# Loads and stores of a row softmax as two transfers each, of the even and of the odd partitions

## The chip, the core and the metric

The kernel runs on one core of a Trainium2 chip. The core has engines of its own for different work: VectorE (DVE in the profile), ScalarE (ACT), GpSimd (POOL) and SyncE (SP), which here does nothing but issue transfers and wait. Data moves between the large memory (DRAM, or HBM) and the core's on-chip memory, which has 128 partitions, by 16 DMA engines. The metric is the time of one execution on the device in microseconds; the number that counts is the median of several executions.

## What is computed

A softmax over the last axis of a float32 tensor of 16 x 1024 x 512, so 16384 rows of 512 numbers each:

```python
def reference(x):
    x_max = np.max(x, axis=-1, keepdims=True)
    exp_x = np.exp(x - x_max)
    return exp_x / np.sum(exp_x, axis=-1, keepdims=True)
```

The input is 33.55 MB and so is the output. Nothing can be kept on the chip from one execution to the next, so 67.11 MB have to be moved.

## The kernel before

**Tiles.** A "group" is 8 softmax rows in each of the 128 partitions: 128 x 4096 float32, 2 MB. There are 16 groups (`GROUPS`). The on-chip memory holds a ring of 12 groups (`ring`), and group g lives at place g % 12. Beside it stand two small tiles: `stat`, which holds the negated row maximum and later the row's sum, and `recip`, its reciprocal.

**Transfers.** `LOADS` and `STORES` both say that a transfer moves two groups, 4 MB. There are 8 loads (L0 to L7) and 8 stores (S0 to S7). `in_dram` gives the piece of DRAM that belongs to a transfer: 2048 consecutive softmax rows, which are dealt to the partitions in order, 16 rows to each. So partition p has one run of 32 KB in memory, and the runs of the 128 partitions follow one another. All transfers are issued on SP's queue (`load` in line 127, `store` in line 131).

**Order on SP.** The first six loads are issued at once; the very first is moved ahead of the start barrier (`AT_HEAD`, `loads_at_the_head`). Then the string `ORDER` rules: S0 S1 L6 L7 S2 S3 S4 S5 S6 S7. A store waits until both of its groups are scaled (semaphore `scaled[k]`). L6 and L7 write over places of the ring that S0 and S1 have read, so they wait for the landing of these stores (semaphore `stored[k]`). The last line on SP waits for the landing of all other stores (`others`).

**A landing.** Each transfer adds 16 to its semaphore by the time that it has landed. Line 144 makes DVE wait for 16 on `loaded[k]` before it reads the groups of load k.

**Compute.** The string `SEQUENCE` is the order on DVE, and on POOL. `M3` is the row maximum of group 3, `MM4` that of groups 4 and 5 in one instruction (line 145). `D3` is the scaling of group 3 on DVE, `P4` that of group 4 on POOL: a reciprocal on DVE (line 159), then a multiply (line 161), whose engine is chosen by the letter. ACT runs a loop over the groups (line 134): for each of the 8 rows, an exponential with the sum of the row beside it. Each row is worked on inside its partition; nothing crosses partitions.

Of the kernel before, what the change touches and what calls it, by code (L numbers as in the profile page):

```python
# [15 lines left out]
GROUP = 8  # L16
# [4 lines left out]
STORES = [2, 2, 2, 2, 2, 2, 2, 2]  # L21
GROUPS = sum(LOADS)
LOAD_AT = [sum(LOADS[:k]) for k in range(len(LOADS))]
STORE_AT = [sum(STORES[:k]) for k in range(len(STORES))]

ORDER = """
S0 S1 L6 L7 S2 S3 S4 S5 S6 S7
# [32 lines left out]
@with_exitstack  # L60
def kernel(
    ctx: ExitStack,
    tc: tile.TileContext,
    x: bass.AP,
    out: bass.AP,
):
    nc = tc.nc
    nc.at_finalize(loads_at_the_head)
    P = nc.NUM_PARTITIONS

    x_rows, out_rows = x.flatten_outer_dims(), out.flatten_outer_dims()
    d = x_rows.shape[1]
    assert x_rows.shape[0] == P * GROUPS * GROUP

    def sbuf(name, n):
        return ctx.enter_context(nc.sbuf_tensor(name, [P, n], F32))

    ring = sbuf("ring", RING * GROUP * d)

    stat = sbuf("stat", RING * GROUP)  # L80
    recip = sbuf("recip", RING * GROUP)

    def sem(name):
        return ctx.enter_context(nc.semaphore(name))

    maxima, summed, inverted = [sem(s) for s in ("maxima", "summed", "inverted")]
    loaded = [sem(f"loaded{k}") for k in range(len(LOADS))]
    scaled = [sem(f"scaled{k}") for k in range(len(STORES))]

    def load_of(g):  # L90
        return max(k for k in range(len(LOADS)) if LOAD_AT[k] <= g)

    def store_of(g):
        return max(k for k in range(len(STORES)) if STORE_AT[k] <= g)


    before = {
        k: store_of(LOAD_AT[k] + LOADS[k] - 1 - RING)
        for k in range(len(LOADS))
        if LOAD_AT[k] >= RING  # L100
    }

    awaited = sorted(set(before.values()))
    stored = {k: sem(f"stored{k}") for k in awaited}
    others = sem("others")

    def at(g):
        return g % RING

    def rows(g, groups=1):  # L110
        part = ring[:, at(g) * GROUP * d : (at(g) + groups) * GROUP * d]
        return part.rearrange("p (r d) -> p r d", d=d)

    def cols(t, g, groups=1):
        return t[:, at(g) * GROUP : (at(g) + groups) * GROUP]

    def in_dram(t, g, groups):
        k = load_of(g)
        assert load_of(g + groups - 1) == k
        part = t[P * GROUP * LOAD_AT[k] : P * GROUP * (LOAD_AT[k] + LOADS[k]), :]  # L120
        first = (g - LOAD_AT[k]) * GROUP
        part = part.rearrange("(p r) d -> p r d", p=P)
        return part[:, first : first + groups * GROUP, :]

    def load(k):
        g, n = LOAD_AT[k], LOADS[k]
        return nc.sync.dma_start(out=rows(g, n), in_=in_dram(x_rows, g, n))

    def store(k):
        g, n = STORE_AT[k], STORES[k]  # L130
        return nc.sync.dma_start(out=in_dram(out_rows, g, n), in_=rows(g, n))

    def exp(row, one):
        return nc.scalar.activation(  # L134
            out=row, in_=row, func=EXP, bias=one, scale=1.0, accum_out=one
        )

    def spread(t):
        return t.unsqueeze(2).to_broadcast([P, GROUP, d])


    def rowmax(g, groups):
        assert load_of(g) == load_of(g + groups - 1)
        nc.vector.wait_ge(loaded[load_of(g)], 16)  # L144
        nc.vector.reduce_max(  # L145
            out=cols(stat, g, groups), in_=rows(g, groups), axis=AX, negate=True
        ).then_inc(maxima, groups)

    def exps():
        with nc.Fori(0, GROUPS, 1, engines=(ACT,)) as g:  # L150
            nc.scalar.wait_ge(maxima, 1).then_inc(maxima, -1)  # L151
            row = nc.scalar.snap((g % RING) * GROUP)
            for r in range(GROUP):
                done = exp(ring[:, bass.ds((row + r) * d, d)], stat[:, bass.ds(row + r, 1)])
            done.then_inc(summed, 1)

    def scale(g, engine):
        nc.vector.wait_ge(summed, g + 1)
        nc.vector.reciprocal(out=cols(recip, g), in_=cols(stat, g)).then_inc(inverted, 1)  # L159
        engine.wait_ge(inverted, g + 1)  # L160
        engine.tensor_mul(  # L161
            out=rows(g), in0=rows(g), in1=spread(cols(recip, g))
        ).then_inc(scaled[store_of(g)], 1)

    def done_by(k):
        later = [a for a in awaited if a >= k]
        return stored[later[0]] if later else others

    def store_scaled(k):
        nc.sync.wait_ge(scaled[k], STORES[k])  # L170
        store(k).then_inc(done_by(k), 16)


    with tc.manual_schedule(engines={SP}):
        for k in range(min(before)):
            first = load(k).then_inc(loaded[k], 16)
            tc.info.no_tile_sem_insts.add(first.ins.name)
    tc.close()
    tc.compile()  # L179

    nc.scalar.preload_act_table(EXP)  # L181
    exps()
    for work in SEQUENCE.split():
        kind = work.rstrip("0123456789")
        g = int(work[len(kind) :])
        if kind in ("M", "MM"):
            rowmax(g, len(kind))
        else:
            scale(g, nc.vector if kind == "D" else nc.gpsimd)
    for transfer in ORDER.split():  # L190
        k = int(transfer[1:])
        if transfer[0] == "S":
            store_scaled(k)
        else:
            last = before[k]
            since = max([a for a in awaited if a < last], default=-1)
            nc.sync.wait_ge(stored[last], 16 * (last - since))
            load(k).then_inc(loaded[k], 16)
    nc.sync.wait_ge(others, 16 * (len(STORES) - 1 - max(awaited)))
    nc.sync.nop()  # L200


# [28 lines left out]
```

## Time and profile before

| what | us |
|---|---|
| median of 3 runs (159.95 to 160.03) | 160.0 |
| the profiled execution, its own time | 160.08 |
| its span, from the first to the last instruction | 158.8 |
| DVE busy | 121.8 |
| ACT busy | 92.2 |
| POOL busy | 42.3 |
| row maximum of one group on DVE (L145) | 4.42 |
| row maximum of two groups on DVE | 8.65 |
| multiply of one group on DVE, median (L161) | 4.425 |
| multiply of one group on POOL (L161) | 7.016 |
| one exponential on ACT (L134), of 128 x 512 | 0.707 |
| issue to landing, median: loads, stores | 25.9, 24.0 |

How to read it: a time "busy" is the sum over an engine's instructions. The span is cut into 40 equal slices for the row of digits, where 9 means that an engine (or the 16 DMA engines in the mean) was busy for 90% or more of the slice. From issue to landing counts the wait in the queue behind earlier transfers too, so it is not how long a transfer takes. A DMA packet here is one row of 32 KB of one partition, or a small one at the end of a transfer.

### The profile page before, as it was taken

How to read it: one execution, taken by the hardware profiler on the slowest of the kernel's cores; microseconds unless marked ns; L12 is line 12 of the kernel's file. 1: busy time of each engine (PE TensorE's matmuls, PEld its weight loads, DVE VectorE, ACT ScalarE, POOL GpSimd, SP SyncE). 2: the span in 40 equal slices, each digit the busy share in tenths (PEclk: the TensorE clock that was granted, in tenths of full speed). 3: DMA queues.
4: the chain of work that ended last, by engine and by line, in shares of the span. 5: the costliest groups of instructions: out<-in, count | busy, mean ns of one | idle time of the engine just before them, and what ended most of it. 6: DMA issues, size and time to landing. Idle time of an engine off the chain costs nothing.

```text
span 158.8 us, 572 instructions
## 1 busy us (share of the span) xinstructions
DVE 121.8 (77%) x36; ACT 92.2 (58%) x257; POOL 42.3 (27%) x10
## 2 busy tenths in 40 slices
DVE  0008979999999999999999499999999999700000
ACT  0300699969406999999988990899599300000000
POOL 0000000000007903930970790079049300000000
DMA  7999999999999999999999999999999999999996
GB/s 264 438 479 405 405 495 421 396 438 471 413 405 438 471 405 396 396 413 471 438 396 462 446 413 405 454 421 438 438 421 446 413 446 438 438 421 438 429 429 264
DMA packets 2304, 67.11 MB, mean 423 GB/s; under 512 B 256, under 2 KB 256, under 8 KB 256
## 3 DMA queue, kind: packets, MB, share of 16 engines
q1 hardware_dynamic: 2304, 67.11, 98.9%
HBM read 33.55 MB, written 33.55 MB: 423 GB/s over the span
## 4 chain that ended last, share of the span: by engine, by line
DMA 45%; DVE 39%; issue 2%; DVEq 0%
DMA ring<-in_x_dram 26%; DVE ring L161 22%; DMA out_dram<-ring 20%; DVE stat L145 16%; DVE recip L159 1%; DVEq L144 0%
## 5 line engine op out<-in xcount | busy, mean ns | idle before, releaser
L134 ACT ACTIVATE ring<-ring,stat x128 | 90.4, 707 | 28.1 <-ACTq L151 28.1
L145 DVE TENSOR_REDUCE stat<-ring 128x16 f32<-128x8192 f32 (+1 forms) x10 | 69.5, 6956 | 15.7 <-DMA ring<-in_x_dram 15.7
L161 POOL TENSOR_TENSOR ring<-ring,recip 128x4096 f32<-128x4096 f32 x6 | 42.1, 7016 | 81.8 <-DVE recip L159 81.8
L161 DVE TENSOR_TENSOR ring<-ring,recip 128x4096 f32<-128x4096 f32 x10 | 51.1, 5109 | 0.3
L134 ACT ACTIVATION_READ_ACCUMULATOR ring<-ring,stat x128 | 23.8, 186 | 0.0
L181 ACT ACT_TABLE_LOAD x1 | 1.3, 1283 | 4.0 <-PEq L179 4.0
L159 DVE RECIPROCAL recip<-stat 128x8 f32<-128x8 f32 x16 | 3.0, 190 | 0.0
L215 POOL MEMSET const-float32-0.0<- 128x1 f32 x1 | 0.1, 98 | 0.2 <-issue 0.2
L215 POOL MEMSET const-bfloat16-1.0<- 128x1 bf16 x1 | 0.1, 102 | 0.0
L215 POOL MEMSET const-uint8-127<- 128x1 uint8 x1 | 0.1, 102 | 0.0
L215 POOL MEMSET const-float32-1.0<- 128x1 f32 x1 | 0.1, 98 | 0.0
## 6 DMA issues: line engine op xcount, KB each, us to landing
ring<-in_x_dram SPq DMA_DIRECT2D x8, 4096.0 KB, 25.9
out_dram<-ring SPq DMA_DIRECT2D x8, 4096.0 KB, 24.0
```

The source lines that it names most:

```text
L134: return nc.scalar.activation(out=row, in_=row, func=EXP, bias=one, scale=1.0, accum_out=one)
L145: nc.vector.reduce_max(out=cols(stat, g, groups), in_=rows(g, groups), axis=AX, negate=True).then_inc(maxima, groups)
L159: nc.vector.reciprocal(out=cols(recip, g), in_=cols(stat, g)).then_inc(inverted, 1)
L161: engine.tensor_mul(out=rows(g), in0=rows(g), in1=spread(cols(recip, g))).then_inc(scaled[store_of(g)], 1)
L181: nc.scalar.preload_act_table(EXP)
L215: nc = _bacc.Bacc("TRN2", target_bir_lowering=False, num_devices=1)
```

## The change

A new list, `PIECES`, says into how many transfers each load is cut: two, for all eight. `in_dram` cuts the 4 MB of a load into two halves that are each in one piece in memory, 1024 softmax rows, and deals the rows of half j, still 16 to a partition, to the 64 partitions j, j + 2, j + 4 and so on. So half 0 goes to the even partitions and half 1 to the odd ones. Before, partition p had the run number p of the 4 MB; now an even partition p has run p / 2, and an odd one run 64 + (p - 1) / 2. A run is 32 KB as before. A store takes the same way back, with the same cut, so the output is where it was.

Both halves of a load add 16 to the same semaphore, and those who waited for 16 wait for 32; the waits for stores are counted in the same manner by `store_count`. The order of the loads and stores, the ring and all compute stay as they are. `AT_HEAD` still moves one transfer of SP ahead of the start barrier, which is now the first half of L0.

```diff
+PIECES = [2, 2, 2, 2, 2, 2, 2, 2]
...
-        part = part.rearrange("(p r) d -> p r d", p=P)
-        return part[:, first : first + groups * GROUP, :]
-
-    def load(k):
+        n = PIECES[k]
+        part = part.rearrange("(n q r) d -> n q r d", n=n, q=P // n)
+        return [part[j, :, first : first + groups * GROUP, :] for j in range(n)]
+
+
+    def load(k, done):
         g, n = LOAD_AT[k], LOADS[k]
-        return nc.sync.dma_start(out=rows(g, n), in_=in_dram(x_rows, g, n))
-
-    def store(k):
+        ones = [
+            nc.sync.dma_start(out=rows(g, n)[j :: PIECES[k]], in_=part).then_inc(done, 16)
+            for j, part in enumerate(in_dram(x_rows, g, n))
+        ]
+        return ones
+
+    def store(k, done):
         g, n = STORE_AT[k], STORES[k]
-        return nc.sync.dma_start(out=in_dram(out_rows, g, n), in_=rows(g, n))
+        by = PIECES[load_of(g)]
+        for j, part in enumerate(in_dram(out_rows, g, n)):
+            nc.sync.dma_start(out=part, in_=rows(g, n)[j::by]).then_inc(done, 16)
+
+    def store_count(first, last):
+        return 16 * sum(PIECES[load_of(STORE_AT[k])] for k in range(first, last))
...
-        nc.vector.wait_ge(loaded[load_of(g)], 16)
+        nc.vector.wait_ge(loaded[load_of(g)], 16 * PIECES[load_of(g)])
...
-        store(k).then_inc(done_by(k), 16)
+        store(k, done_by(k))
...
-            first = load(k).then_inc(loaded[k], 16)
-            tc.info.no_tile_sem_insts.add(first.ins.name)
+            for one in load(k, loaded[k]):
+                tc.info.no_tile_sem_insts.add(one.ins.name)
...
-            nc.sync.wait_ge(stored[last], 16 * (last - since))
-            load(k).then_inc(loaded[k], 16)
-    nc.sync.wait_ge(others, 16 * (len(STORES) - 1 - max(awaited)))
+            nc.sync.wait_ge(stored[last], store_count(since + 1, last + 1))
+            load(k, loaded[k])
+    nc.sync.wait_ge(others, store_count(max(awaited) + 1, len(STORES)))
```

## The prediction

> **What bounds the kernel now.** I read the busy table and the slices of the span first.
>
> ```profile
> span 158.8 us, 572 instructions
> ...
> DVE 121.8 (77%) x36; ACT 92.2 (58%) x257; POOL 42.3 (27%) x10
> ...
> DMA  7999999999999999999999999999999999999996
> ...
> q1 hardware_dynamic: 2304, 67.11, 98.9%
> ```
>
> No compute engine is busy for more than 77% of the span. The 16 DMA engines are busy from the first slice to the last, and their packets fill 98.9% of 16 engines' span. So the transfers bound the kernel. The 45% DMA in the chain of waits understates this: the chain passes through DVE work while the DMA engines are still draining loads issued long before. The unit of that work comes from the chain in order of time and the waits for line 145: the first load is there at 12.37 us, and the second ends the next DMA piece at 22.03.
>
> ```profile
> 0.79 21.24 DMA ring<-in_x_dram
> 22.03 0.02 issue
> 22.05 4.42 DVE stat L145
> ```
>
> A 4 MB transfer therefore takes 22.05 - 12.37 = 9.68 us. It has 128 partition rows of 32 KB, eight for each DMA engine, so a row takes 1.21 us. Sixteen transfers are 16 x 9.68 = 154.9 us. What is left of the span, 3.9 us, is the start (12.37 - 9.68 = 2.7 us), a dip at the change from loads to stores, and the last landing. The packet count agrees: 2304 is 16 x (128 rows + 16 small ones, one for each engine).
>
> Next, is it the memory, in one direction, or the engines? The windows answer (columns: stretch, length, busy DVE, ACT, POOL, clock, DMA share, GB/s):
>
> ```profile
> 20.00:50.00 30.00, 29.00 (x10) 21.07 (x60) 1.28 (x1) 1.00 1.00 431
> 57.00:60.00 3.00, 2.97 (x3) 3.00 (x9) 0.00 (x0) 1.00 1.03 350
> 110.00:156.00 46.00, 27.67 (x10) 12.51 (x36) 8.17 (x2) 1.00 1.00 433
> ```
>
> Loads alone run at 431 GB/s, stores alone at 433. One limit serves both directions, so it is at the DMA engines or at their way into the on-chip memory, and each engine has 27 GB/s of it. The dip at 57 us costs 3 x (1 - 350/431) = 0.56 us. Last, the DMA view of the first 12 us, in slices of 0.3 us:
>
> ```profile
> DMA  0009920007950595059505950295029502970299
> GB/s 0 0 0 874 765 109 0 0 0 328 1201 218 0 218 1311 218 0 218 1311 218 0 218 1311 218 0 109 1420 218 0 109 1420 218 0 109 1311 328 0 109 1092 437
> ```
>
> A packet's bytes are counted in one slice, so this shows a beat: every four slices, 1.2 us, the engines change rows together, three quarters of them or more inside one slice (1311 of 1747, then 1420). They march in step and do not drift apart. The same view from 40 to 52 us still has this beat; from 110 to 122 us it is smeared over the whole period.
>
> **The change, part by part.** *Issues.* 16 more, at a median of 0.40 us (line 127) and 0.34 us (line 131): 8 x 0.40 + 8 x 0.34 = 5.9 us of SP's queue. What hides them is waiting: SP waits 112.0 us for scaled groups and 39.2 us for landings. Only the first piece now goes out ahead of the start barrier; it is four rows, 4.8 us of DMA work, and the six loads before took 3.17 us to issue altogether, so the second piece comes long before the first is through. Cost 0; without cover, one issue before the last store would cost 0.34 us. Queued behind each second piece is the next wait of SP, which in this order of stores and loads has tens of us to spare.
>
> *Completions.* 256 more small packets, 16 for each engine. From above, all idle DMA time (1.1% of 158.8 us = 1.75 us) belongs to the 16 present boundaries, and 16 more cost as much again. From below 0: the beat passes 11 to 12 us, where one load follows the other, unbroken. I take 0.1 us, near the beat's row.
>
> *Wait counts and layout in memory.* The waits for 32 in place of 16 release on the same last landing. A row is softmaxed inside its partition, so which rows meet in a partition changes no compute. Memory still gives 32 KB runs; since reads and writes reach the same rate, I cost the new order in memory at 0, and bound a gain by the 3.9 us outside of the rows.
>
> *64 partitions in a transfer.* This is the term that decides. Each engine now has four rows per transfer in place of eight. If 64 rows are dealt in order, engine e gets rows 4e to 4e+3, that is every second partition from 8e to 8e+7, first two from one group of four partitions and then two from the next. Nothing in the trace shows which way into the on-chip memory a partition uses. It shows only that with 128 partitions, all 16 engines keep 27 GB/s at once. From below the price is 0: every engine still has a way of its own. From above, two engines in step want the same way while other ways stand idle, and each row takes twice its 1.21 us: +154.9 us. The nearest row for two users that meet at the ring's memory is that of line 161:
>
> ```profile
> L161 DVE TENSOR_TENSOR ring<-ring,recip x10: 4424/4425/11273, 26.6 to 133.4; 128x4096 f32<-128x4096 f32 x10
> L161 POOL TENSOR_TENSOR ring<-ring,recip x6: 7016/7016/7017, 48.7 to 117.4; 128x4096 f32<-128x4096 f32 x6
> ```
>
> The one multiply of DVE that starts beside POOL's (117.39 against 117.37 us) takes 11.27 us, nearly 7.02 + 4.42: one was served after the other, in full. The row of the 128-partition transfers speaks for the low end, but it stands for eight rows per engine out of a full set of partitions, which is what this edit gives up. I take the high end less what the phase saves. If one of a pair is ahead by d, then in a section of two rows (2.42 us) the two meet for only 2.42 - d, and the factor is 2 - d/2.42. While the beat is sharp (loads 0 to 5) d is half a slice, 0.15 us, factor 1.94; smeared over a period of 1.2 us, d is on average a third of it, 0.4 us, factor 1.83. (6 x 1.94 + 10 x 1.83)/16 = 1.87; the last pair ends the kernel, so 1.88.
>
> [...]
>
> *Sum.* 154.9 x 0.88 = 136.3 us, plus 0.1, on the profiled execution's 160.08 us (its span is 158.8, so 1.3 us lie around it; it stands 0.08 above the median): 296.5, or 296 us on the median of 160.0. No other engine gets late: loads land every 18.2 us, and DVE, busy for 121.8 us in all, waits more. L6 waits for S0's landing, but S1 is then still queued, so the DMA engines do not run dry.
>
> **The rivals.** *No meeting.* The deal leaves each engine its own way. [...] Then only completions remain: 160.1 us, at most 1.75 us more. This decides if the first load, both halves, is there by 12.4 us. The same case with a visible boundary cost gives 160.3 to 162, a little slower.
>
> *Faster, by a shorter start or turn.* Place: the 2.7 us before the row time of load 0 and the 0.56 us dip at 57 us. A piece with half the rows is ready sooner by up to half of the longest issue (524 ns), 0.26 us, and the turn may cost half: 160.0 - 0.26 - 0.28 + 0.1 = 159.6. It decides once these savings exceed 16 boundary costs, at 0.034 us each. Against it: rows themselves at 1.21 us leave nothing.
>
> *Half a meeting.* Only loads or only stores meet, or the pairs slip out of step. One direction: 8 x 9.68 x 0.88 = 68 us, 228 us. Slipping: once a partner is ahead by 2.42 us both run free; the smear after 57 us is what speaks for it, the unbroken beat before speaks against. If it came after the six loads, 6 x 9.68 x 0.94 = 55 us, 215 us.
>
> *A fixed price for each transfer.* [...] The trace disagrees: two loads follow at 9.68 us, eight rows at the beat's period, with no gap. I leave it inside the case before.
>
> **How the numbers follow.** Meeting in both directions 0.50 (own range 284 to 315, factors 1.8 to 2.0); half a meeting 0.13 (162 to 284); no meeting 0.16 within 0.2% and 0.12 from 160.3 to 162; faster 0.09. A measurement of this kernel tells no more than about 0.2%, 0.32 us, from no change. So slower 0.50 + 0.13 + 0.12 = 0.75, same 0.16, faster 0.09. To leave out no more than 2 in 10, the range must reach from the case of no meeting to the upper bound: 159.7 to 315, which leaves out most of faster.
>
> **What would show it.** Right: the second load's landing 18 us or so after the first, a beat of 2.4 us in the DMA view of the first stretch, some 230 GB/s while the DMA share stays at 9, DVE waiting at every load, the durations of compute unchanged. Wrong: a beat that stays at 1.2 us (no meeting); slow stretches of one direction alone (half); gaps in the DMA row at every transfer's end (fixed price); SP issues that come after the DMA row has gone empty (my cover for the issues).

## The result, and the profile after

| | median us | range | runs |
|---|---|---|---|
| before | 159.97 | 159.75 to 160.57 | 20 |
| changed | 160.84 | 160.20 to 161.28 | 20 |

The ratio is 1.0049, with a 95% interval of 1.0037 to 1.0061: the change costs 0.9 us, not 136. The profiled execution of the changed kernel took 160.3 us, so it shows the milder end of the range. First its page:

```profile
span 159.0 us, 588 instructions
...
DVE 121.8 (77%) x36; ACT 92.3 (58%) x257; POOL 42.3 (27%) x10
...
DMA  8999999999999999999999999999999999999996
...
DMA packets 2560, 67.11 MB, mean 422 GB/s; under 512 B 512, under 2 KB 512, under 8 KB 512
```

The change is there: 2560 packets are the 2048 rows and 512 small ones, 16 for each of 32 transfers. The DMA engines are as full as before. The windows (columns as in the prediction) and the DMA view of the first 12 us show the rate and the beat:

```profile
20.00:50.00 30.00, 28.96 (x10) 21.04 (x59) 0.73 (x1) 1.00 1.01 436
...
110.00:156.00 46.00, 28.09 (x10) 12.93 (x38) 8.60 (x2) 1.00 1.00 433
```

```profile
DMA  0000999300099509950795059502950299029902
GB/s 0 0 0 0 655 546 437 109 0 0 0 655 874 218 0 437 1092 218 0 328 1201 218 0 218 1311 218 0 109 1420 218 0 109 1092 546 0 109 1092 546 0 109
```

Loads alone run at 436 GB/s and stores alone at 433 (431 and 433 before). The beat is still four slices of 0.3 us from the second row on; the first row takes some seven slices, before and after. So no row shows the doubled time, 2.42 us, expected of two engines that meet. The second load, which the prediction put 18 us after the first, is there 9.72 us after it (22.60 less 12.88 us):

```profile
2.42 20.16 DMA ring<-in_x_dram
22.57 0.02 issue
22.60 4.42 DVE stat L158
```

What did move is the beginning. The same view in slices of 0.06 us, first of the kernel before, then of the changed one:

```profile
DMA  0000000000000000099999900000900000000000
```

```profile
DMA  0000000000000000000000999990009900009000
```

The first engines begin their first row in slice 22 in place of 17, 0.30 us later, and the last one in slice 36 in place of 28, 0.48 us later. DVE's wait for load 0 ends at 12.88 us in place of 12.37 (timelines before and after):

```profile
12.37 4.42 DVE L145 TENSOR_REDUCE stat<-ring 128x8 f32<-128x4096 f32 x1 [12.37 <-DMA ring<-in_x_dram]
```

```profile
12.88 4.42 DVE L158 TENSOR_REDUCE stat<-ring 128x8 f32<-128x4096 f32 x1 [12.88 <-DMA ring<-in_x_dram]
```

The issues that lead there are in the rows of SP's two load lines, before and after (shortest, median, longest in ns):

```profile
L127 SPq DMA_DIRECT2D ring<-in_x_dram x8: 333/404/524, 0.0 to 81.1; - x8
```

```profile
L132 SPq DMA_DIRECT2D ring<-in_x_dram x16: 471/598/921, 0.0 to 82.1; - x16
```

Here a transfer of 64 rows took longer to issue than one of 128: 598 ns against 404 at the median.

### The profile page after: what moved, and what is told of

Its sections match the earlier page's. It is cut to its first block, busy times and chain, and to the rows that moved or that the text cites. A ratio compares the mean times of both kernels' runs of the same rounds, so it can differ in the third digit from the quotient of the medians.

```text
span 159.0 us, 588 instructions
## 1 busy us (share of the span) xinstructions
DVE 121.8 (77%) x36; ACT 92.3 (58%) x257; POOL 42.3 (27%) x10
## 2 busy tenths in 40 slices
DMA packets 2560, 67.11 MB, mean 422 GB/s; under 512 B 512, under 2 KB 512, under 8 KB 512
## 3 DMA queue, kind: packets, MB, share of 16 engines
q1 hardware_dynamic: 2560, 67.11, 98.7%
## 4 chain that ended last, share of the span: by engine, by line
DMA 44%; DVE 39%; issue 2%; SPq 1%; DVEq 0%
DMA ring<-in_x_dram 24%; DVE ring L174 22%; DMA out_dram<-ring 19%; DVE stat L158 16%; SPq L132 1%; DVE recip L172 1%; SPq L141 0%; DVEq L157 0%
```

## The experiments

Theory after the result: the meeting of engines is real, but even and odd partitions are dealt so that it doesn't occur; the 0.9 us come from the start. The rivals: there is no meeting in any deal, and each of the 16 more transfers has a small price. Each run is set beside the kernel before as run on the same chip with it.

**e1, the lower and the upper 64 partitions.** In the load, and likewise in the store:

```diff
-            nc.sync.dma_start(out=rows(g, n)[j :: PIECES[k]], in_=part).then_inc(done, 16)
+            nc.sync.dma_start(out=rows(g, n)[j * (P // PIECES[k]) : (j + 1) * (P // PIECES[k])], in_=part).then_inc(done, 16)
```

> The two transfers are of partitions 0 to 63 and 64 to 127 in place of even and odd ones; each is still 2 MB in one piece. Theory of the meeting (engines that share a way into the on-chip memory slow each other; the even and odd cut happened to avoid it): with the halves the beat of the DMA view goes to about 2.4 us and the time to 250 to 315 us. Theory that there is no meeting in any dealing of 64 rows: the beat stays at 1.21 us and the time at 160.2 to 161.3 us, as with even and odd.

Measured: 269.44 us (four executions, 261.14 to 276.51) against 159.97. A window and the first 14 us of the DMA view, in slices of 0.35 us:

```profile
20.00:50.00 30.00, 15.70 (x5) 13.62 (x39) 0.00 (x0) 1.00 1.00 210
```

```profile
DMA  0005997009999000999900049999000899900499
```

The beat is now seven slices, 2.45 us, twice the row of 1.21, and loads run at 210 GB/s with a DMA share of 1.00: all engines are occupied, each at half its rate. So the doubled row that the prediction expected of a meeting exists, and with no saving by phase: 436/210 is a factor of 2.08 in loads. That two engines share a way there is my reading of it; no run shows the way itself. Stores suffer less: with all loads landed by 195.5 us, they run at 341 GB/s from 200 to 220 us and at 377 from 220 to 240, and the 16 engines are then far out of step (the last 16 landings spread over 12 us). That is how the prediction's slipping pairs would look, but no run tests it by itself.

**e5, 64 partitions from 32 to 95.** The kernel before, with load 1 in three transfers:

```diff
+WHOLE = [(0, 128)]
+CUTS = {1: [(32, 96), (0, 32), (96, 128)]}
...
```

> The kernel before, with load 1 alone cut in three: partitions 32 to 95 first (64 of them), then 0 to 31 and 96 to 127. It asks how the rows of a 64-row transfer are dealt to the engines. [...] Theory of dealing in order, four neighbouring rows to each engine: no two engines meet in 32 to 95, a beat of 1.2 us there for four rows, and only the outer two cost 2.4 us more each: 165 us. Theory that groups are halved (an engine takes rows 2e, 2e + 1 and the same two 16 rows on, which gives even and odd partitions their own ways): engines meet two by two, the beat in 32 to 95 is 2.4 us: 170 us.

Measured: 164.39 us against 160.00, ratio 1.0274 (1.0254 to 1.0295). The DMA view from 12 to 24 us, where load 1 runs:

```profile
DMA  0297029700970099000099990000499900009995
GB/s 0 109 1311 328 0 109 1311 328 0 0 1420 328 0 0 1311 437 0 0 0 0 655 655 218 218 0 0 0 0 109 765 546 328 0 0 0 0 218 874 437 109
```

The rows of partitions 32 to 95 keep the beat of four slices, 1.2 us (their first began before this window); from slice 14 on come the outer pieces, whose rows take six to nine slices, about 2.4 us. So the count of 64 rows is harmless here, and what matters is which partitions they are. Of the two theories, dealing in order forecast this beat and 165 us, halved groups a beat of 2.4 us and 170. Both rest on my assumption of which partitions share a way, which no run shows. And under that assumption dealing in order would let even and odd partitions meet, as the prediction had it, but their beat stayed at 1.2 us. So under it neither deal fits both measurements; how rows are dealt, and what engines share, stays open.

**e2, e3, e4: the start or each transfer.** Only the list is edited, one line for each kernel in this order:

```diff
-PIECES = [2, 2, 2, 2, 2, 2, 2, 2]
+PIECES = [1, 2, 2, 2, 2, 2, 2, 2]
...
+PIECES = [2, 1, 1, 1, 1, 1, 1, 1]
...
+PIECES = [4, 4, 4, 4, 4, 4, 4, 4]
```

> Load 0 and store 0 are one transfer again, all others are still two. Theory of the start (the first load lands 0.52 us later, 12.86 against 12.34 us, because its second piece is issued after the first and each issue takes some 0.6 us): most of the loss goes, 160.0 to 160.3 us. Theory of a price for each transfer (0.87 us over 16 more transfers is 0.054 us each): 14 of 16 stay, 160.7 us.

> Only load 0 and store 0 are two transfers. Theory of the start: 160.4 to 160.9 us, the first load's landing again some 0.5 us late. Theory of a price for each transfer: 2 of 16 more, 160.1 us.

> Four transfers of every fourth partition, 32 partitions each, 48 more transfers than before. Theory of a price for each transfer at 0.054 us: 160.0 + 48 x 0.054 = 162.6 us. Theory of the start: the first load lands when its fourth piece has been issued; if issues keep some 0.6 us each and two rows per engine take 2.4 us, the start is no later than with two pieces, and the time is 160.3 to 161.2 us.

Measured, against 159.97: first load whole 160.24 (ratio 1.0007 to 1.0037); only the first cut 160.68 (1.0029 to 1.0059), both as the theory of the start had it; four pieces 161.73 (1.0090 to 1.0161), above what that theory had and below 162.6. One cut at the start costs 0.7 us, and undoing it takes two thirds of the loss away. The price for each transfer falls as the main cause. But with the first load whole, five of 12 executions lay between 160.59 and 160.99, the others at 160.25 or below: with the four pieces' excess, something besides the start was left.

**e6, e7: the order in memory, and stores alone.** e6 cuts the same partitions, but each keeps its old run:

```diff
-        part = part.rearrange("(n q r) d -> n q r d", n=n, q=P // n)
+        part = part.rearrange("(q n r) d -> n q r d", n=n, q=P // n)
```

e7 has this too, and a second list that keeps all loads whole:

```diff
+LOAD_PIECES = [1, 1, 1, 1, 1, 1, 1, 1]
...
```

> Even and odd partitions as in the change, but each partition keeps the run of memory that it had before, so that a transfer reads every second 32 KB run and is no longer in one piece. Theory that one piece in memory is neither gain nor loss: as the changed kernel, 160.5 to 161.1 us. Theory that the order in memory makes up the part of the loss that is not the start: 160.4 us or less; or, if one piece is a gain, above 161.3 us.

> Loads whole as before, each store two transfers of even and odd partitions (every second run of memory). Theory of the start: the first load lands as before, at 12.3 to 12.4 us, and the time is 159.9 to 160.2 us. Theory of a price for each transfer in the middle or at the end (0.054 us each, or a tail that waits for the second issue): 160.4 us or more.

Measured, against 160.00: e6 160.46 (160.30 to 160.64; ratio 1.0018 to 1.0037), between the figures of the two theories, and 0.4 us under the changed kernel; e7 160.11 (0.9994 to 1.0016), not to be told from no change. Cut stores cost no more than 0.16%, in the old order, and the "one piece in the memory" looks like a loss. In e6, the first rows begin as late as in the change (slice 22), but DVE has load 0 at 12.48 us, not at 12.88.

**e8, e10: four pieces in both orders.** Load 0 and store 0 whole, all others in four; e8 in the new order, e10 with e6's line:

```diff
-PIECES = [2, 2, 2, 2, 2, 2, 2, 2]
+PIECES = [1, 4, 4, 4, 4, 4, 4, 4]
```

> Load 0 and store 0 whole, all others in four transfers of every fourth partition: 42 more transfers than before, and none of them first. Theory of the start: of the 1.76 us that four pieces cost, 1.4 us go with the first load's landing, and 42 transfers at 0.01 us stay: 160.1 to 160.5 us. Theory of a price for each transfer of 0.02 us or more: 160.8 us or more.

> As the kernel with the first load whole and the others in four, with the memory order of before. It took 161.09 us in the new order. Theory that the order in memory makes the loss behind the start: 160.0 to 160.35 us. Theory of a price for each transfer (42 or 84 more of them at about 0.02 us): 160.8 to 161.2 us.

Measured: e8 161.09 against 160.00 (1.0049 to 1.0079), so the start alone was wrong; e10 160.54 against 159.95 (1.0024 to 1.0050). About half of e8's loss goes away with the old order. The rest, 0.59 us over 42 loads and stores more (three more for each of 14), is 0.014 us each, between the two expectations.

**e9, e11, e12: closing the sum, and where.** e9 is e6 with load 0 whole; e11 is the changed kernel with loads 0, 6 and 7 whole; e12 is the changed kernel again.

```diff
-PIECES = [2, 2, 2, 2, 2, 2, 2, 2]
+PIECES = [1, 2, 2, 2, 2, 2, 2, 2]
...
+PIECES = [1, 2, 2, 2, 2, 2, 1, 1]
```

> Load 0 and store 0 whole, the other 14 transfers of each cut into even and odd partitions, every partition with the run of memory that it had before (so no piece is in one piece). Theory of two costs (0.5 us at the start, some 0.35 us from the new order in memory): both are gone here, 159.9 to 160.15 us. Theory of a start and a price for each transfer: the price of 14 or 28 more transfers stays, 160.25 us or more, as with the first load whole in the new order (160.24).

> The changed kernel with load 0, loads 6 and 7 and their stores whole again (whole transfers have the memory order of before). In the profiles of two kernels with the new order, one engine falls behind the others by some 1 us while load 6 follows on store 1, about 81 to 86 us. Theory that this turn from stores to loads is where the new order costs: 159.9 to 160.15 us. Theory that it costs everywhere or at the first turn, at 57 us: 160.2 us or more.

> The changed kernel once more, so that it stands beside the other three on the same chip. Theory of two costs: 160.7 to 161.0 us, and if its profile shows an execution above 160.7 us, one engine lands its last transfers more than 1 us behind the first, where the earlier profile (an execution of 160.3 us) shows 0.8 us. Theory that the gap to the old order in memory (160.46) was a matter of the chip: 160.4 to 160.6 us.

Measured, against 159.95: e9 160.16 (1.0006 to 1.0027), at the edge of "two costs"; e11 160.20 (1.0003 to 1.0021), at the edge of "everywhere or at the first turn". Both are some 0.2 us above before. By its median, e11 is only 0.04 us under e2, which has loads 6 and 7 cut in the new order too; but none of its 11 executions is above 160.29, and five of e2's 12 are above 160.5. So in this pair what the last two carry is the slow tail. e12 took 160.96 (1.0044 to 1.0085), up to 162.20, as "two costs" had it. e12's profile caught an execution of 161.55 us. The end, from 154 to 160 us in slices of 0.15, of the kernel before and of e12:

```profile
DMA  0959999559599595995990000000000000000000
```

```profile
DMA  9999055099990550999905500000005000000000
GB/s 437 874 1311 437 0 218 218 0 437 655 1529 437 0 218 218 0 437 437 1748 437 0 218 218 0 0 0 0 0 0 0 218 0 0 0 0 0 0 0 0 0
```

In e12, all but one engine begin their last row by 157.3 us (slice 21), and a single row (218 GB/s is one row of 32 KB in 0.15 us) begins at 158.5, slice 30. One engine is behind the rest by more than a row's time, and the kernel ends when it does. Part of that is from the start: in the same trace, the last engine to begin its fifth row is 0.78 us behind the middle one of the 16, and 0.76 us behind in the 47th row, the sixth load's, so nothing is made up on the way.

**e13, e14, e15: the cut without the new order, and the new order at one turn.** Load 6 is the first load behind stores. e13 and e15 have e6's line, e14 the new order:

```diff
-PIECES = [2, 2, 2, 2, 2, 2, 2, 2]
+PIECES = [2, 1, 1, 1, 1, 1, 1, 1]
...
+PIECES = [1, 1, 1, 1, 1, 1, 2, 2]
```

> Only load 0 and store 0 are cut into even and odd partitions, with the memory order of before; with the new order the same cut took 160.68 us. Theory that the order in memory delays the first rows of a stream of loads: the first load lands at some 12.4 us and the time is 160.1 to 160.35 us. Theory that the cut alone does it (the longer issue of the first piece): 160.5 us or more.

> Only loads 6 and 7 and stores 6 and 7 are cut, in the new order: load 6 is the first load behind stores. Theory that the new order costs where a stream of loads begins: some executions lose 0.4 us or more, the slowest quarter above 160.5 us, median 160.1 to 160.7 us. Theory that only the very first load matters: 159.95 to 160.15 us and none above 160.4 us.

> The same two loads and stores cut, with the memory order of before. Theory that the order costs at the turn: none of the losses of the new order, 159.95 to 160.15 us. Theory that cutting there costs whatever the order: as in the new order, 160.2 us or more where that has it.

Measured, against 159.89: e13 160.38 (1.0021 to 1.0049), between its theories, so the cut of load 0 costs some 0.5 us without any new order; e14 160.32 (1.0022 to 1.0049), as a steady shift rather than the tail expected; e15 159.92 (0.9996 to 1.0014), nothing. e14 and e15 differ in the order alone: 0.4 us for the new order of two loads and two stores. Their traces point to the load for a part of it. From the second to the third row of load 6, at about 82 to 84 us, the last of the 16 engines falls back by 0.28 us in e14, 0.45 in e2 and 0.84 in e8, all in the new order; in e6, e9, e10 and e15, which cut load 6 in the old order, by 0.01 at most. In the new order it does not happen each time: the changed kernel's trace and e12's show nothing there, and e4's 0.09.

**The loss, then:** the cut in the old order costs 0.46 us (e6), of which 0.21 stay when load 0 is whole (e9), and the changed kernel, which differs from e6 in the order alone, loses 0.4 to 0.55 us more (0.87 and, in e12, 1.01 in all). At load 0 the profiles show the new order: DVE has a whole load 0 at 12.15 to 12.48 us, a cut one at 12.48 (e6) and 12.56 us (e13) in the old order, and at 12.88, 13.01 (e3) and 13.26 us (e12) in the new. Where else it costs is not settled. Pairs of kernels that differ in it alone, each taken against its own kernel before, differ by 0.50 us (e8 and e10) and 0.40 (e14 and e15), clear of noise, and by 0.22 (e3 and e13) and 0.06 (e2 and e9), which are not. The parts do not add either: e13, with one load and one store cut, loses as much as e6 with all. I take this to be because the end is that of the slowest engine, so that delays on different engines hide one another; that is argued, not shown. What in the memory holds an engine up in the new order is not in these records and stays open. No kernel tried was faster than before.

## Why the prediction was wrong, point by point

**The bound was right.** The DMA engines bound the kernel (their packets fill 98.9% of 16 engines' span before and 98.7% in the changed kernel), and the busy times of DVE, ACT and POOL did not move: 121.8, 92.2 and 42.3 us before, 121.8, 92.3 and 42.3 after.

**The step that failed** is the term of the 64 partitions. It begins with "If 64 rows are dealt in order, engine e gets rows 4e to 4e+3" and takes the high end of its price, +154.9 us, at which each row takes twice its 1.21 us. That deal, its groups of four partitions and a way that two engines share were assumptions of mine; no run shows any of them. What the runs show in their place: even and odd partitions cost nothing per row, the beat stayed at 1.21 us, and loads at 436 GB/s; 32 to 95 kept the beat too (e5); and the doubled row itself was no fancy, for e1 has it, 2.45 us, when a transfer has the lower or the upper half of the partitions alone. Which premise is false, the deal in order or the way that engines would share, stays open. I should have seen that the row for the low end stood for transfers like these ones: a set of partitions that spreads over the whole memory. The multiply of line 161, which I took as nearest, showed DVE's taking 11.27 us in place of 4.42 beside POOL's, not that transfers slow each other. The saving by phase (1.88 in place of 2) was wrong as well where the beat is sharp: e1's loads are at 2.08. Only e1's stores, far out of step, are below it (433/341 and 433/377, 1.27 and 1.15).

**The rival that held** was "no meeting" with a visible cost, 160.3 to 162 us, to which I gave 0.12. What came out is its sign and its range, but its price was for the wrong thing: boundary costs. These I had at 0.1 us for 16; e10's 0.014 us each would make 0.22 for 16, and e9 has 0.21 for 14. The rest of the 0.9 us is the start and the order in memory.

**"Cost 0" for the issues** was wrong at one place. The cover that I named, SP's waits, is not there at the very first one, ahead of which there is nothing; behind it, e7 with all stores cut took 160.11 us and e9 with all but load 0 and store 0 cut 160.16. And I priced 64-row issues by the 128-row rows (0.40 and 0.34 us) where they take 0.60 and 0.59 at the median. I also noted that the second piece comes early enough, which it did; it is the first that is late. Of the 39.2 us for landings, 20.6 are SP's last wait, which comes behind all issues and covers none.

**"I cost the new order in memory at 0"** was wrong, by some 0.4 us (e6 and the changed kernel). My argument, the equal steady rates of loads and stores (431 and 433 GB/s before, 436 and 433 in the changed kernel), is one about the middle of a stream. It says nothing of the first rows, where a cut load 0 came 0.3 to 0.8 us later in the new order than in the old, and an engine held up there did not catch up (in e12 it was 0.78 us behind, and 0.76 after six loads).

**Faster by a shorter start** went the other way: half the rows did not make the first piece ready sooner; its first rows began 0.30 us later. Nor did the turn to stores get shorter: from 57 to 62 us the DMA engines moved 380 GB/s before and 360 in the changed kernel. The 350 GB/s on which the prediction's dip of 0.56 us rests are just 32 rows begun in 3 us; in the changed kernel the same 3 us have 426, so a window that short can't size a dip.

## What to carry to other kernels

Before pricing a transfer of fewer partitions, ask which partitions it names, not only how many: every second one ran at the full rate here (loads at 436 GB/s), the lower and the upper half at half of it (210). In this kernel, whose transfer engines are full from end to end, the first issue was on the path and nothing behind it made up for it (e13, with the old order and load 0 and its store cut, lost 0.5 us), so in one like it leave the first transfer in the form that is issued fastest. And judge such a kernel by its last engine: e12's mean share of 97.9% hides one that is a row behind.

## What the runs showed of the hardware that was not expected

A load of 64 rows took longer to issue than one of 128 rows, 0.60 us at the median against 0.40, and so did one of 32: with four pieces, the 24 transfers of the first six loads took 15.99 us to issue, 0.67 each. ACT and DVE did not begin until that was done, at 17.03 and 17.07 us. In the timeline of that kernel:

```profile
0.00 15.99 SPq L132 DMA_DIRECT2D ring<-in_x_dram  x24
17.03 1.28 ACT L194 ACT_TABLE_LOAD   x1 [17.03 <-PEq L192]
17.07 13.07 DVE L158 TENSOR_REDUCE stat<-ring 128x8 f32<-128x4096 f32 x3 [17.07 <-PEq L192]
```

ACT's table load was at 3.97 us in the kernel before and is at 9.23 us in the changed one, where load 0 still comes later, at 12.88. And a more compact order in memory was slower, by 0.4 us where two of eight loads and stores had it (e14 and e15; in e2 and e9 the difference is not clear of noise), while the rate within streams was the same to about 1% (loads 436 GB/s in the changed kernel and 431 before, stores 433 in both).
